# A gather's second half moved to another accumulator bank, and a branch hint for the tensor engine

## The chip, the cores and the metric

The kernel runs on one core of a Trainium2 chip. The metric is the device time of one execution in microseconds (us); a measurement is the median of several runs. One further execution is recorded by the hardware profiler, and every row shown here comes from such a record.

## What is computed

One layer of a decoder block for 512 tokens of width 1024, in float32:

```python
h = modulate(rms_norm(x, norm1_g), shift1, scale1)        # scales from the vector c
q, k, v, u, gates = split(h @ w_in)
x = x + gate1 * ((g_attn * (attention @ w_proj_attn) + g_ssm * (ssm @ w_proj_ssm)) @ w_out)
h = modulate(rms_norm(x, norm2_g), shift2, scale2)
# hierarchical mixture of experts: best of 4 groups, then best 2 of its 8 experts
hid = xb @ w_e_in[e]                # 32 experts, each 1024 x 1024
a, g = split(hid)
ys = (silu(a) * g) @ w_e_out[e]     # each 512 x 1024
x = x + gate2 * sum(weight * ys)
out = rms_norm(x, final_g)
```

The first two thirds of the text of the kernel compute the attention and state-space branches. The change is in the mixture of experts, the last 530 us of the execution.

## The kernel before

**Experts in pairs.** The 32 experts are worked through as 16 pairs, p = 0 to 15, with 64 places (CAP) for tokens in each expert. The weights of a pair come as 12 loads of 1 MiB (1,048,576 bytes): eight of `w_ein` (128 rows of both experts each) and four of `w_eout`. They go through a ring of 17 slots in the order in which they are used, so a load can be issued when the work that read the same slot 17 loads earlier has ended. `fetch` issues them on SyncE's queue.

**One pair on the tensor engine.** The order on TensorE and SyncE is the order of the program text (a manual schedule). VectorE and ScalarE are ordered by the framework's planner, until the last pair, from where they follow the text too. For each pair p TensorE does:

1. `hid_mm`, eight steps k: the pair's gathered tokens (`xT`) times `w_ein`, into `hid[0]` and `hid[1]`, which are PSUM banks 0 and 1.
2. `give(p - 1, ys[0], ...)`: four token blocks of the previous pair's first output half are put back to their tokens (8 matmuls, banks 4 to 7). VectorE adds them to x.
3. `gather`: the tokens of coming pairs are picked with a 0/1 matrix P (matmuls `xg`). One call of `gather` does one half of the width (four of the eight blocks of 128) for two pairs at once. Its output has two halves of 512 columns, and a half fills one bank: 16 matmuls, then a VectorE copy and a ScalarE copy into `xT`, one for each pair.
4. between the two halves, `act_turned`: four transposes of the activated `hid`, in bank 0, copied out by VectorE.
5. `places`: four small matmuls `ix` that find, for each place, its token and weight.
6. `give(p - 1, ys[1], ...)`, and then `yb_mm`: the second product, into `yb`, which is the tile `pair` on banks 2 and 3.

`gather` is called twice at p = 0 (both halves for pairs 1 and 2) and once at each of p = 1 to 12; at p = 13 it is called twice for the one pair that is left, where one bank holds the whole output (n = 1). In the kernel before, both halves of a call lie in one tile `both` on banks 2 and 3:

```python
both = pair((128, 2, per_bank, 128 * n) if n == 2 else (128, 2, 2, 128), name="xg")
for k0 in range(0, 4, per_bank):
    xg = both[:, k0 // per_bank] if n == 2 else both.rearrange("p a b c -> p (a b) c")
```

The framework places the waits between engines: an instruction that writes a PSUM tile waits for the ones that read what it overwrites, and two engines that read one tile are put one after the other. `places` has its output in bank 1.

**The end.** After pair 14 the last pair's `hid_mm` is interleaved with `give`, and its activation is transposed (L1540) and copied into `hT` by VectorE and ScalarE (L1541). Then every engine loads one number, the largest count of tokens of an expert (L1545), and branches on it (L1546): if a count is over 64, the body `overflow()` is run, a loop over all experts; here it is jumped over. The code behind the branch computes the last pair's output in five pieces (`piece`, matmuls `yq`, L1561), puts it back to the tokens, and normalizes and stores the result.

Of the kernel before, what the change touches and what calls it, by code (L numbers as in the profile page):

```python
# [20 lines left out]
KC = D // 128  # L21
NT = T // 128
NE = 32
CAP = 64
# [33 lines left out]
def hybrid_block(ctx: ExitStack, tc: tile.TileContext, x, cols, cst, ada_a, ada_b, b_rows, bc_rows, lamv, relb,  # L58
                 onehot, units, rw, rb, bpad, cpad, w_ein, w_eout, out):
    nc = tc.nc  # L60
    V, S, G, TE = nc.vector, nc.scalar, nc.gpsimd, nc.tensor
# [5 lines left out]
    def bank(i, shape=(128, 512), name=None):  # L67
        return psum.tile(list(shape), F32, tag=f"b{i}", name=name or f"bank{i}")
# [8 lines left out]
    def t1(tag, shape, dt=F32, name=None):  # L77
        pool = late if tag[:-1] == "tmp" else mid if tag[:-1] in ("BT", "CT", "sgA", "xs") else early
        return pool.tile(list(shape), dt, tag=tag, name=name or tag)
# [9 lines left out]
    def tt(o, a, b, op, eng=None):  # L89
        return emit(o, lambda: (eng or V).tensor_tensor(o, a, b, op=op))  # L90

    def ts(o, a, s1, op0, s2=None, op1=None, eng=None):
        return emit(o, lambda: (eng or V).tensor_scalar(o, a, s1, s2, op0=op0, **({"op1": op1} if op1 is not None else {})))  # L93
# [99 lines left out]
    def pair(shape=(128, 2, 512), name="pair"):  # L193
        return psum.tile(list(shape), F32, tag="b23", name=name)
# [324 lines left out]
    with tc.manual_schedule(engines={mybir.EngineType.PE, mybir.EngineType.DVE, mybir.EngineType.Activation}):  # L519
# [16 lines left out]
        for k in range(KC):  # L536
            first, second = unit_parts(UNITS[k]) if k in UNITS else (lambda: None, ) * 2
            for n in range(3 * 6):

                m, w = (n // 2, n % 2) if n < 12 else (n - 12, 2)  # L540
                b = 6 * k + m
# [431 lines left out]
    for i in range(4):  # L973
        m2s = []
        for m in (2 * i, 2 * i + 1):
# [5 lines left out]
            a = t1(f"u{m % 2}", [128, T], name="ma")  # L981
            b = t1(f"u{2 + m % 2}", [128, T], name="mb")
# [173 lines left out]
    def xg_mm(o, P, k, i, w, start):  # L1156

        TE.matmul(o, (h2h, h2l)[w][i][:, 128 * k:128 * k + 128], P[:, i].rearrange("p a b -> p (a b)"), start=start,  # L1158
                  stop=i == NT - 1 and w == 1, skip_group_check=True)
# [59 lines left out]
    with tc.manual_schedule(engines={mybir.EngineType.PE}):  # L1219
# [10 lines left out]
        for i in range(NT):  # L1230
            ps = bank((5, 0, 1, 0)[i], name="po2")
            n = T if i < 3 else 256
            for s_ in range(KC * T // n):
                k, c0 = s_ % KC, n * (s_ // KC)
# [14 lines left out]
    NP = NE // 2  # L1249
    ring = {}  # L1250
    nring = [-1]

    def slot(name, n=None, t=F32):
        if n is None:
            n = nring[0] = nring[0] + 1
        return p2r.tile([128, 2, D], t, tag=f"r{FREED[n % RING]}", name=name)
# [59 lines left out]
    xT, held, left = {}, {}, ["x0", "x1", "x2", "x3"]  # L1316

    def x_half(p, h):
        held[p, h] = left.pop(0)
        xT[p, h] = p2.tile([128, 4, 128], F32, tag=held[p, h], name="xT")  # L1320
        return xT[p, h]

    def gather(ps, P, h, between=None):

        n, per_bank = len(ps), 4 // len(ps)
        to = [x_half(p, h) for p in ps]
        both = pair((128, 2, per_bank, 128 * n) if n == 2 else (128, 2, 2, 128), name="xg")
        for k0 in range(0, 4, per_bank):
            xg = both[:, k0 // per_bank] if n == 2 else both.rearrange("p a b c -> p (a b) c")
            for kk in range(per_bank):  # L1330
                for i in range(NT):
                    for w in range(2):
                        xg_mm(xg[:, kk], P, 4 * h + k0 + kk, i, w, i == w == 0)
                if between and kk == 1 and k0 == 0:
                    between()
            for j in range(n):
                (V.tensor_copy, S.copy)[(j + k0 // per_bank) % 2](to[j][:, k0:k0 + per_bank], xg[:, :, 128 * j:128 * j + 128])  # L1337

    def places(p, P, j=0):

        ix = bank(1, (128, 6), "ix")
        for i in range(NT):
            TE.matmul(ix, P[:, i, 2 * j:2 * j + 2].rearrange("p a b -> p (a b)"), cwt[:, i, p], start=i == 0, stop=i == NT - 1)
        ws = p2.tile([128, 8], F32, tag="ws", bufs=4, name="ws")
        V.tensor_copy(ws[:, 0:6], ix)
        for e in range(2):
            r = slice(64 * e, 64 * e + 64)
            tt(ws[r, 6:7], ws[r, 2 * e:2 * e + 1], ws[r, 2 * e + 1:2 * e + 2], OP.add)
        ts(ws[:, 7:8], ws[:, 4:5], -1.0, OP.add)
        disp[p] = [ws]  # L1350
# [7 lines left out]
    def act(hid):  # L1358
        a = p2.tile([128, 512], F32, tag="hT", name="sa")
        S.activation(a, hid[0], AF.Silu)  # L1360
        tt(a, a, hid[1], OP.mult)
        return a
# [23 lines left out]
    def give(p, y, i, q, b):  # L1386

        ps = bank(b, name="cb")
        give_mm(p, y, i, ps)
        add(i, 512 * q, ps)  # L1390

    def hid_mm(p, hid, k):
        for q in range(2):
            for e in range(2):
                TE.matmul(hid[q][64 * e:64 * e + 64], xT[p, k // 4][:, k % 4, 64 * e:64 * e + 64], ring[p][k][:, e, 512 * q:512 * q + 512],  # L1395
                          start=k == 0, stop=k == KC - 1, skip_group_check=True)

    def yb_mm(p, yb, hT_, f):
        for q in range(2):
# [61 lines left out]
    for p in range(NP - 1):  # L1461
# [4 lines left out]
        hid = [bank(q, name="hid") for q in range(2)]  # L1466
        for k in range(KC):
            hid_mm(p, hid, k)
        a = act(hid)
# [4 lines left out]
        if p == 0:  # L1474
            with tc.issue_after(last[0].ins), tc.issue_after(last[1].ins):
                weights()
                P = chosen(1, 2)
            places(0, P0)
# [5 lines left out]
        if p == 0:  # L1484
            gather((1, 2), P, 0, act_turned)
            gather((1, 2), P, 1)
            places(1, P, 0)
            places(2, P, 1)
        elif p < NP - 3:
            if p % 2:  # L1490
                P = chosen(p + 2, 2)
                gather((p + 2, p + 3), P, 0, act_turned)
            else:
                gather((p + 1, p + 2), P, 1, act_turned)
            places(p + 2, P, 1 - p % 2)
        elif p == NP - 3:
            P = chosen(NP - 1, 1)
            gather((NP - 1, ), P, 0, act_turned)
            gather((NP - 1, ), P, 1)
            places(NP - 1, P)  # L1500
        else:
            act_turned()
# [11 lines left out]
    hid = [bank(q, name="hid") for q in range(2)]  # L1514
    for k in range(4):
        hid_mm(NP - 1, hid, k)
# [5 lines left out]
                                                  mybir.EngineType.Activation}))  # L1522

    for k in range(4, KC):
        hid_mm(NP - 1, hid, k)
        if k < KC - 1:
            for n in ((0, 1), (2, 3), (4, 5))[k - 4]:
                give(NP - 2, ys[n // 4], n % 4, n // 4, 4 + n % 2)
    a = slot("sa", free[0] + 3)[:, 0, :512]
# [13 lines left out]
        add(2 + j, 512, pl[j])  # L1543
    back(NP - 1, slot("PT", free[0] + 10, F32R)[:, 0, :512])
    ov = nc.values_load(ci[0:1, 0:1], min_val=0, max_val=2 * T)  # L1545
    with tc.If(ov > CAP):  # L1546
        overflow()

    PIECES = ((0, 256), (256, 256), (512, 256), (768, 128), (896, 128))
# [232 lines left out]
```

## Time and profile before

| | |
|---|---|
| median of 3 runs | 972.01 us (970.54 to 976.26) |
| the profiled execution's own time | 972.46 us |
| its span, first to last instruction | 970.3 us (2.16 us lie around it) |
| TensorE (PE) busy | 917.0 us, 95% |
| VectorE (DVE), ScalarE (ACT) busy | 501.4 us, 300.8 us |
| mean granted TensorE clock | 0.971 of full speed |
| moved by DMA | 267.66 MB |

In rows of the profile, PE stands for matmuls and PEld for TensorE's weight loads, PEq and PEldq for instructions of its sequencer. A row of a timeline has the start in us, the duration in us, the engine, the line, the operation with output and inputs, shapes and a count; what stands in brackets at its end is how long the engine had been idle before, and what ended that. Matmuls overlap: the next one starts before the one before has ended, so the distance of two starts is what one costs.

### The profile page before, as it was taken

What the parts mean: (1) busy time and instruction counts of PE and PEld (TensorE: products, weight loads), DVE (VectorE), ACT (ScalarE), POOL (GpSimd) and SP (SyncE); (2) the same over time, 40 slices, a digit from 0 to 9 for tenths busy, and PEclk for the clock granted to TensorE, in tenths of its full rate; (3) what the DMA queues carried; (4) which work ended last, traced back from release to release, by engine and by line L of the source; (5) the groups of instructions that cost most, each with busy time, mean ns of one, the idle gap of its engine ahead of it and who ended that gap; (6) DMA issues with size and microseconds to landing.
All of it is one profiled execution on the core that took longest, in us unless ns stands there. A gap on an engine that the chain in (4) does not pass through costs nothing. (4 is left out here: it accounts for less than half of the span.)

```text
span 970.3 us, 13070 instructions
## 1 busy us (share of the span) xinstructions
PE 917.0 (95%) x5060; PEld 571.3 (59%) x5060; DVE 501.4 (52%) x1249; ACT 300.8 (31%) x615; POOL 7.2 (1%) x12
## 2 busy tenths in 40 slices
PE   8997997989999999998899999999999999999985
PEld 5775764777877787786535553455544555446334
DVE  8886866756656565487204333343323444224236
ACT  4574588875545332243101010010100101000014
POOL 0000000000000000000000000000000000000002
PEclk9997998999999999997989999999999999999997
DMA  9925665421223433925878999999999999999902
GB/s 364 352 88 208 235 215 212 169 66 66 77 76 130 163 120 126 417 108 209 312 300 334 417 417 420 418 419 419 420 418 420 418 420 420 419 420 373 361 2 87
DMA packets 77189, 267.66 MB, mean 276 GB/s; under 512 B 5503, under 2 KB 11551, under 8 KB 77124
## 3 DMA queue, kind: packets, MB, share of 16 engines
q1 hardware_dynamic: 77124, 266.78, 70.4%
q8 instruction: 42, 0.69, 0.3%
q14 instruction: 23, 0.19, 0.1%
HBM read 264.64 MB, written 3.17 MB: 276 GB/s over the span
## 5 line engine op out<-in xcount | busy, mean ns | idle before, releaser
L1395 PE MATMUL hid<-w,xT 128*64 128x512 f32 x1024 | 225.2, 597 | 0.0
L1395 PEld LDWEIGHTS hid<-w,xT 128*64 128x64 f32 x1024 | 73.4, 138 | 146.5 <-issue 146.0
L1401 PE MATMUL yb<-w,sa 128*64 128x512 f32 x480 | 110.8, 616 | 0.0
L90 DVE TENSOR_TENSOR sa<-sa,hid 128x512 f32<-128x512 f32 (+1 forms) x17 | 11.1, 657 | 162.7 <-PE hid L1395 151.7
L90 DVE TENSOR_TENSOR wl<-ws,wh 128x1024 fp32r<-128x1024 f32 x52 | 63.5, 1222 | 55.0 <-ACT wh L153 44.3
L90 DVE TENSOR_TENSOR x<-x,cb 128x512 f32<-128x512 f32 (+1 forms) x132 | 79.9, 664 | 5.4 <-PE cb L1380 5.4
L180 PE MATMUL acc<-hh,wh 128*128 128x512 f32 x176 | 74.3, 422 | 4.4 <-ACT wh L153 4.4
L153 ACT ACTIVATE wh<-ws 128x1024 fp32r<-128x1024 f32 x51 | 53.7, 1057 | 78.1 <-PE acc L180 24.4
L1373 ACT CAST yh<-yf 128x512 fp32r<-128x512 f32 x29 | 18.0, 619 | 193.2 <-DVE yf L96 163.7
L1158 PE MATMUL xg<-P,mh 128*128 128x256 f32 (+1 forms) x288 | 67.7, 288 | 9.7 <-ACT xT L1337 7.3
L1401 PEld LDWEIGHTS yb<-w,sa 128*64 128x64 f32 x480 | 34.2, 141 | 68.7 <-issue 66.8
L180 PE MATMUL acc<-hl,wh 128*128 128x512 f32 x176 | 71.3, 405 | 0.0
L180 PE MATMUL acc<-hh,wl 128*128 128x512 f32 x176 | 71.1, 405 | 0.0
L96 DVE SCALAR_TENSOR_TENSOR yf<-yb,ws,gate 128x512 f32<-128x512 f32 x29 | 21.8, 751 | 90.8 <-PE yb L1401 90.3
L1158 PE MATMUL xg<-P,ml 128*128 128x256 f32 (+1 forms) x288 | 66.0, 282 | 0.0
L1360 ACT ACTIVATE sa<-hid 128x512 f32<-128x512 f32 x15 | 9.0, 597 | 169.5 <-PE hid L1395 169.5
L1158 PEld LDWEIGHTS xg<-P,mh 128*128 128x128 f32 x288 | 52.9, 192 | 13.9 <-ACT xT L1337 10.6
L1158 PEld LDWEIGHTS xg<-P,ml 128*128 128x128 f32 x288 | 53.0, 193 | 0.5
L1380 PE MATMUL cb<-yh,PT 128*128 128x512 f32 x116 | 48.4, 417 | 0.1
L1380 PE MATMUL cb<-yl,PT 128*128 128x512 f32 x116 | 45.8, 395 | 1.5 <-DVE yl L90 1.4
L180 PEld LDWEIGHTS acc<-hh,wh 128*128 128x128 f32 x176 | 34.0, 193 | 14.2 <-ACT wh L153 4.7
L180 PEld LDWEIGHTS acc<-hh,wl 128*128 128x128 f32 x176 | 33.9, 192 | 9.4 <-issue 1.6
(308 smaller groups left out, 1434.7 us busy)
## 6 DMA issues: line engine op xcount, KB each, us to landing
w<-w_ein SPq DMA_DIRECT2D x128, 1024.0 KB
w<-w_eout SPq DMA_DIRECT2D x63, 1024.0 KB
ws<-units SPq DMA_DIRECT2D x52, 512.0 KB
adaw<-ada_b SPq DMA_DIRECT2D x32, 512.0 KB
ada<-ada_a SPq DMA_DIRECT2D x8, 512.0 KB
ada<-ada_a SPq DMA_DIRECT2D x16, 256.0 KB
X<-x SPq DMA_DIRECT2D x4, 512.0 KB
x<-x SPq DMA_DIRECT2D x4, 512.0 KB
```

The source lines that it names most:

```text
L90: return emit(o, lambda: (eng or V).tensor_tensor(o, a, b, op=op))
L96: return emit(o, lambda: V.scalar_tensor_tensor(o, a, s, b, op0=op0, op1=op1, **k))
L153: return (lambda: S.activation(hi, st, AF.Copy) if u else V.tensor_copy(hi, st)), lambda: tt(lo, st, f32(hi), OP.subtract)
L180: TE.matmul(o, a, b, start=start and i == 0, stop=stop and i == 2)
L1158: TE.matmul(o, (h2h, h2l)[w][i][:, 128 * k:128 * k + 128], P[:, i].rearrange("p a b -> p (a b)"), start=start, stop=i == NT - 1 and w == 1 ...
L1360: S.activation(a, hid[0], AF.Silu)
L1373: S.copy(yh, yf)
L1380: TE.matmul(ps, PT if len(y) == 2 else f32(PT), a, start=w == 0, stop=w == len(y) - 1)
L1395: TE.matmul(hid[q][64 * e:64 * e + 64], xT[p, k // 4][:, k % 4, 64 * e:64 * e + 64], ring[p][k][:, e, 512 * q:512 * q + 512], start=k == 0 ...
L1401: TE.matmul(yb[q][64 * e:64 * e + 64], hT_[:, f, 64 * e:64 * e + 64], ring[p][8 + f][:, e, 512 * q:512 * q + 512], start=f == 0, stop=f == ...
```

## The change

- In `gather` the first half is written to a tile on banks 2 and 3 of which only the first bank is used, and the second half to a tile of its own in bank 1. With n = 1 nothing moves: the one output still lies in bank 2.
- In `places` the output `ix` moves from bank 1 to bank 0.
- After the matmuls of step k = 4 of the last pair's `hid_mm`, a hint is placed in TensorE's stream: the branch labelled "overflow" will likely be taken, that is, the body will be jumped over. Only TensorE gets it. `hid_mm` returns its last matmul so that the place can be named.

```diff
@@ gather
-        both = pair((128, 2, per_bank, 128 * n) if n == 2 else (128, 2, 2, 128), name="xg")
         for k0 in range(0, 4, per_bank):
-            xg = both[:, k0 // per_bank] if n == 2 else both.rearrange("p a b c -> p (a b) c")
+            xg = bank(1, (128, per_bank, 128 * n), name="xg") if k0 else pair((128, 8 // n, 128 * n), name="xg")
...
-                (V.tensor_copy, S.copy)[(j + k0 // per_bank) % 2](to[j][:, k0:k0 + per_bank], xg[:, :, 128 * j:128 * j + 128])
+                (V.tensor_copy, S.copy)[(j + k0 // per_bank) % 2](to[j][:, k0:k0 + per_bank], xg[:, :per_bank, 128 * j:128 * j + 128])
@@ places
-        ix = bank(1, (128, 6), "ix")
+        ix = bank(0, (128, 6), "ix")
@@ hid_mm
-                TE.matmul(hid[q][64 * e:64 * e + 64], ...)
+                m = TE.matmul(hid[q][64 * e:64 * e + 64], ...)
+        return m
@@ the last pair
-        hid_mm(NP - 1, hid, k)
+        mm = hid_mm(NP - 1, hid, k)
+        if k == 4:
+            with tc.issue_after(mm.ins):
+                tc.mark_branch_hint_location("overflow", "LikelyTaken", engines=[mybir.EngineType.PE])
...
-    with tc.If(ov > CAP):
+    with tc.If(ov > CAP, label="overflow"):
         overflow()
```

## Rows read from the trace of the kernel before

**Rows 1.** The page: TensorE's busy time and its share of the span.

```profile
PE 917.0 (95%) x5060; PEld 571.3 (59%) x5060; DVE 501.4 (52%) x1249; ACT 300.8 (31%) x615; POOL 7.2 (1%) x12
```

**Rows 2.** Windows: us, PE, PEld, DVE, ACT, POOL busy; granted clock; DMA share; GB/s.

```profile
529.80:859.90 330.10, 324.77 (x1674) 158.24 (x1672) 123.33 (x237) 28.40 (x55) 0.00 (x0) 1.00 1.02 418
...
859.90:920.00 60.10, 57.84 (x300) 27.82 (x298) 20.62 (x36) 3.67 (x6) 0.00 (x0) 1.00 1.00 389
920.00:944.40 24.40, 20.24 (x90) 7.56 (x86) 9.31 (x16) 3.69 (x6) 0.00 (x0) 1.00 0.01 3
```

**Rows 3.** Waits of TensorE: total us, times, longest us.

```profile
PE xg L1158 <- ACT xT L1337: 7.3, 14, 1.0
...
PE xg L1158 <- DVE xT L1337: 1.7, 2, 0.9
...
PE ix L1343 <- DVE sa L90: 0.7, 1, 0.7
```

**Rows 4.** Timeline of one gather's middle, all engines.

```profile
667.40 0.28 PE L1158 MATMUL xg<-P,ml 128*128 128x256 f32 x1
...
667.52 0.60 PE L1302 MATMUL xtp<-colt,sa 128*128 128x128 f32 x4
...
668.15 0.69 DVE L1306 COPY sa<-xtp 128x512 f32<-128x512 f32 x1
668.18 0.37 ACT L1337 COPY xT<-xg 128x256 f32<-128x256 f32 x1 [1.89 <-DVE xT L1337]
...
668.60 0.38 PE L1158 MATMUL xg<-P,mh 128*128 128x256 f32 x1 [0.49 <-ACT xT L1337]
668.83 0.28 PE L1158 MATMUL xg<-P,ml 128*128 128x256 f32 x1
...
672.32 0.42 DVE L1337 COPY xT<-xg 128x256 f32<-128x256 f32 x1
```

**Rows 5.** Timeline of TensorE in the two gathers at p = 0.

```profile
475.39 0.28 PE L1158 MATMUL xg<-P,ml 128*128 128x256 f32 x1
...
476.59 0.38 PE L1158 MATMUL xg<-P,mh 128*128 128x256 f32 x1 [0.92 <-DVE xT L1337]
...
478.46 0.28 PE L1158 MATMUL xg<-P,ml 128*128 128x256 f32 x1
...
479.72 0.38 PE L1158 MATMUL xg<-P,mh 128*128 128x256 f32 x1 [0.98 <-ACT xT L1337]
```

**Rows 6.** Timeline around the start of hid(13): TensorE, then VectorE.

```profile
859.95 13.90 PE L1395 MATMUL hid<-w,xT 128*64 128x512 f32 x64
```

```profile
861.65 0.69 DVE L90 TENSOR_TENSOR yl<-yf,yh 128x512 fp32r<-128x512 f32 x1 [0.74 <-ACT yh L1373]
```

**Rows 7.** Lines L1545 and L1546 on the sequencers: ns min/median/max, start us.

```profile
L1545 PEldq TENSOR_LOAD <-ci x1: 488/488/488, 939.7 to 939.7; - x1
```

```profile
L1546 PEldq COMPARE_BRANCH  x1: 3767/3767/3767, 940.3 to 940.3; - x1
...
L1546 ACTq COMPARE_BRANCH  x1: 50/50/50, 940.9 to 940.9; - x1
```

**Rows 8.** Timeline on both sides of the branch.

```profile
940.19 0.42 DVE L1541 COPY hT<-xtp 128x256 f32<-128x256 f32 x1 [0.52 <-PE xtp L1540]
...
944.39 5.36 PE L1561 MATMUL yq<-w,hT 128*64 128x256 f32 x32 [4.02 <-PEq L1546]
...
950.83 1.95 PE L1561 MATMUL yq<-w,hT 128*64 128x256 f32 x16
```

**Rows 9.** Windows of 2 us, columns as in rows 2.

```profile
488.00:490.00 2.00, 2.00 (x8) 0.71 (x6) 0.00 (x0) 0.00 (x0) 0.00 (x0) 0.50 0.00 0
...
946.00:948.00 2.00, 2.00 (x13) 1.36 (x11) 0.48 (x1) 0.14 (x1) 0.00 (x0) 0.50 0.00 0
...
950.00:952.00 2.00, 2.00 (x20) 1.51 (x20) 1.34 (x5) 0.96 (x4) 0.00 (x0) 1.00 0.00 0
```

**Rows 10.** DMA queues from 930 to 931 us: packets, MB, share of 16 engines.

```profile
q8 instruction: 1, 0.02, 8.4%
```

More of the change, by code (lines that the diff above doesn't have):

```diff
@@ L1394, in hid_mm @@
             for e in range(2):
-                TE.matmul(hid[q][64 * e:64 * e + 64], xT[p, k // 4][:, k % 4, 64 * e:64 * e + 64], ring[p][k][:, e, 512 * q:512 * q + 512],
-                          start=k == 0, stop=k == KC - 1, skip_group_check=True)
+                m = TE.matmul(hid[q][64 * e:64 * e + 64], xT[p, k // 4][:, k % 4, 64 * e:64 * e + 64], ring[p][k][:, e, 512 * q:512 * q + 512],
+                              start=k == 0, stop=k == KC - 1, skip_group_check=True)
+        return m
     def yb_mm(p, yb, hT_, f):
```

## The prediction

> **What bounds the kernel now.** I read the page first, then the windows of the mixture of experts, the waits of TensorE, the timeline of one gather, and last the rows around the branch. TensorE is busy for 95% of the span [rows 1]. From 529.80 to 859.90 us, which are eleven pairs of 30.0 us each, it is busy for 324.77 of 330.10 us at full clock, while the DMA engines are busy all the time too, at 418 GB/s [rows 2]. Two candidates, then, and the reader has to see which one sets the pace. A matmul that lacked its weights would show as TensorE waiting for a DMA; the list of waits has no such row for any expert weight, and its rows for these stages are those of [rows 3].
>
> How far ahead the loads are can be counted. All weights are 16 x 12 = 192 loads of 1.0486 MB, 201.3 MB. After 859.90 us there come 389 GB/s x 60.1 us = 23.4 MB, and then practically nothing [rows 2], so 177.9 MB or 169.7 loads had landed when hid(13) began at 859.95 [rows 6]. Thirteen pairs had used 156. So 13.7 of the ring's 17 slots held weights not yet used. The eleven pairs before took 132 loads, and 418 x 330.1 = 138.0 MB or 131.6 loads came in: the store was 14.1 at their start and hardly moves. The loads keep up, with about 34 us of them in hand (13.7 x 2.5 us). TensorE sets the pace, and time taken out of its stream comes off the end until that store is eaten.
>
> **The gather.** In the middle of a call TensorE stands still, although its next matmuls go to another bank than the one being copied. The last matmul of the first half starts at 667.40 and the four transposes at 667.52, so neighbours are about 0.12 us apart. The second half starts only at 668.60, 0.05 us after the ScalarE copy of the first half has ended (668.18 + 0.37), and that copy had itself waited for VectorE's [rows 4]. The one tile on two banks is what ties the second half to copies of the first. In the list this is the wait of xg for the ScalarE copy, 14 times and 7.3 us [rows 3]: 13 such places and one at p = 0 of another kind.
>
> The price of one place: the transposes start 0.11 apart ((0.60 - 0.27) / 3, the last one's length taken as 0.27), so the second half could start at 667.52 + 4 x 0.11 = 667.96 and starts 0.64 later. Its first matmul then takes 0.23 instead of 0.12, since its weights were not loaded ahead, which is another 0.11. Together 0.75 us; the bare idle time, 0.49, is the lower bound. With a bank of its own nothing holds the second half: bank 1 was `hid[1]`, read by VectorE before the gather began. 13 x 0.75 = 9.75 us (6.4 at the bound).
>
> At p = 0 the second call waits for the copies of the first call's second half, and its own second half for its first: 475.39 to 476.59 and 478.46 to 479.72 [rows 5]. Less the normal 0.12, and with the 0.11 for the first matmul, these are 1.19 and 1.25 us. With banks 2 and 1 in turn, each tile has a whole half (16 x 0.12 = 1.9 us) in which its two copies, 0.8 us together, are done. That is 2.4 us.
>
> **`places` in bank 0.** Its first call, at p = 0, waits 0.7 us for VectorE's read of `hid[1]` [rows 3]; bank 0 is read by ScalarE alone, earlier. I take 0.7 us, between nothing (if another input is as late) and that. Elsewhere bank 0 holds the transposes until VectorE has copied them, at 668.15 + 0.69 = 668.84 [rows 4]. `ix` follows the second half, from then on at about 667.96 + 1.9 = 669.85, so 1.0 us is left and the move is free; if VectorE were later than that, TensorE would wait for the difference. Sum for the first two edits: 9.75 + 2.4 + 0.7 = 12.9 us.
>
> Can it be kept? The store loses 12 x 0.75 = 9 us over the pairs 1 to 12, 3.6 loads at 2.5 us each; what is won at p = 0 moves the loads too, since slots come free earlier. A pair's low point is at the end of its `hid`, where 8 loads are used in 13.9 us and 5.5 come in. 13.7 - 3.6 - 2.5 = 7.6 loads remain. So it can.
>
> **The hint.** The same branch takes 50 ns on ScalarE and 3767 ns on TensorE [rows 7], whose body is the long one. Then `yq` starts, after 4.02 us of idle TensorE [rows 8], 0.3 us behind the end of the branch (940.3 + 3.77 = 944.07). With the code behind the branch at hand, the branch would cost the 0.05 us of the other engines. `yq` needs the first half of `hT`, which VectorE ends at 940.61 [rows 8], and would start at about 940.7: 3.6 us earlier. The trace has no row for a hint. It costs between nothing and, by the number that the same sequencer loads ahead of the branch, 0.49 us [rows 7]; it is executed while matmuls are queued, so I take 0.1. That is 3.5 us.
>
> What is late next? [...] 32 matmuls `yq` take 5.36 us behind the stall, 16 of the same shape 1.95 us at full clock [rows 8]. 5.36 - 3.90 = 1.4 us come back if the pause is only some tenths. Behind it TensorE's chain through the pieces stays the longest, and VectorE and ScalarE are idle up to it. 3.5 + 1.4 = 4.9 us.
>
> [...]
>
> **Sum.** 972.46 - 12.9 - 4.9 = 954.7 us, against the profiled execution's own time, which lies 0.45 us above the median of the runs.
>
> **Rivals.**
> - *The hint buys nothing.* The block fetched at 930 to 931 [rows 10] takes the place of the hinted one, and the branch costs 3.77 us again: 954.7 + 4.9 = 959.6 us. For it speaks that fetch; against it the ten microseconds between the hint and the branch, in which a block can come in.
> - *The loads take over.* The DMA share is 1.02 [rows 2]. If matmuls soon waited for weights, the pairs 1 to 12 would give back their 9 us: 963.7 us. Against it stands the store of 13.7 loads; it would need a store under 3.6 + 2.5 loads.
> - *The two halves stay tied*, by a wait that the list puts down to the wrong copy. Then only the end gains: 972.46 - 4.9 = 967.6 us. Against it: the second half starts 0.05 us behind a copy of the first, and the list puts all 14 waits down to that copy [rows 3].
> - *Slower: bank 1 now holds up `hid`.* The next pair's `hid[1]` must wait for the copies of the second half. VectorE makes its copy at 672.32 [rows 4], some 7 us before the next `hid`; its order is the planner's. If the copy were put behind `yl`, which starts at 861.65 for a `hid` that began at 859.95 [rows 6], `hid` would stall until 861.65 + 0.69 + 0.42 = 862.76. Its third matmul, the first in bank 1, is due at about 860.4, so that is 2.4 us, 14 times: 954.7 + 33.6 = 988 us. It turns the result from 17.8 / 14 = 1.3 us a gather on. Against it: the copy's inputs are ready long before, and nothing in front of it is late.
>
> **How the numbers follow.** The forecast as computed has 0.66, no gain from the hint 0.14, the loads 0.08, halves still tied 0.06, slower 0.03, and 0.03 is for mixtures between the second and the fourth. The forecast's own range is 951 to 958: up to 3.3 us more come off if the stretch around 488 us, at 0.50 clock [rows 9] behind the gathers of p = 0, becomes shorter (6.6 us at half clock lose 3.3); 3.4 us come back if one place is worth only 0.49. The range for the time goes from 950.5 to 964, and takes in the first two rivals. A measurement of this kernel can tell about 0.5%, 4.9 us, from no change; tied halves at 967.6 lie within that, the rest faster: 0.91, 0.06, 0.03.
>
> **What would show it.** Right: the wait of xg for the ScalarE copy is gone from the list but for the single-pair call at p = 13; a pair takes 29.25 us at a DMA share still near 1; the branch row of TensorE is near 0.05 us, `yq` starts some 0.4 us behind the transposes and no stretch behind it is at 0.50. Wrong: matmuls waiting for a DMA of w, `hid` or `ix` waiting for a VectorE copy, a branch of 3.7 us, or a fetch that stalls TensorE between hint and branch.

## The result, and the profile after

The changed kernel takes 959.9 us (median of 6, 957.84 to 960.65), the kernel before 973.6 us in the same series (median of 6). The ratio is 0.9854, with a 95% interval of 0.9829 to 0.9878: 1.2 to 1.7% faster. The time lies in the range of the prediction (950.5 to 964) and above the forecast's own range (951 to 958). The profiled execution took 959.85 us, with a span of 957.7 us.

The waits of TensorE, which answer to [rows 3], three rows from the list: total us, times, longest us.

```profile
...
PE row L1455 <- DVE x L90: 0.8, 1, 0.8
PE yq L1564 <- ACTq L1549: 0.8, 1, 0.8
PE xg L1158 <- DVE xT L1336: 0.8, 1, 0.8
```

The 14 waits for ScalarE's copy are gone, so are the wait of `ix` at p = 0 and one of the two for VectorE's copy. What is left of xg's wait for VectorE's copy is the call for a single pair at p = 13. No `hid` waits for a copy, and no matmul of the experts for a DMA.

The middle of a gather, timeline of all engines, which answers to [rows 4]:

```profile
660.14 0.28 PE L1158 MATMUL xg<-P,ml 128*128 128x256 f32 x1
660.26 0.60 PE L1302 MATMUL xtp<-colt,sa 128*128 128x128 f32 x4
660.46 0.42 DVE L1336 COPY xT<-xg 128x256 f32<-128x256 f32 x1
...
660.61 0.36 PE L1158 MATMUL xg<-P,mh 128*128 128x256 f32 x1
...
660.82 0.28 PE L1158 MATMUL xg<-P,ml 128*128 128x256 f32 x1
...
660.89 0.69 DVE L1306 COPY sa<-xtp 128x512 f32<-128x512 f32 x1
660.92 0.37 ACT L1336 COPY xT<-xg 128x256 f32<-128x256 f32 x1 [1.89 <-DVE xT L1336]
```

The second half starts 0.35 us behind the first transpose, while VectorE's copy of the first half still runs and ScalarE's has not begun; before it was 1.08 us (668.60 - 667.52 [rows 4]). That is 0.73 us a place. The first matmul still takes 0.21 us to the next start (its weight load starts 0.02 us ahead of it, those of the next ones 0.12 us ahead), so the 0.11 that the prediction added for it does not come back; but the second half starts 0.35 us behind the transposes where the prediction had 0.44, which makes up for nearly all of that.

The pairs, by the starts of their `hid` in TensorE's timeline, first of the changed kernel, then of the kernel before:

```profile
525.57 13.90 PE L1394 MATMUL hid<-w,xT 128*64 128x512 f32 x64
...
847.41 13.90 PE L1394 MATMUL hid<-w,xT 128*64 128x512 f32 x64
...
885.86 13.90 PE L1394 MATMUL hid<-w,xT 128*64 128x512 f32 x64
```

```profile
529.79 13.90 PE L1395 MATMUL hid<-w,xT 128*64 128x512 f32 x64
...
893.58 13.90 PE L1395 MATMUL hid<-w,xT 128*64 128x512 f32 x64
```

Eleven pairs, hid(2) to hid(13), take 847.41 - 525.57 = 321.84 us instead of 859.95 - 529.79 = 330.16: 8.32 us, or 0.76 a pair. The windows of that stretch and of the one where time was lost (us, PE, PEld, DVE, ACT, POOL busy; granted clock; DMA share; GB/s):

```profile
525.57:847.41 321.84, 321.84 (x1674) 157.96 (x1672) 123.32 (x237) 28.41 (x55) 0.00 (x0) 1.00 1.02 419
```

```profile
868.00:870.00 2.00, 1.93 (x15) 1.93 (x15) 0.02 (x1) 0.00 (x0) 0.00 (x0) 0.85 1.03 424
870.00:872.00 2.00, 2.00 (x11) 2.00 (x11) 0.00 (x0) 0.00 (x0) 0.00 (x0) 0.50 1.03 424
...
876.00:878.00 2.00, 2.00 (x6) 1.32 (x4) 1.67 (x3) 0.00 (x0) 0.00 (x0) 0.50 1.01 416
878.00:880.00 2.00, 2.00 (x7) 0.68 (x8) 1.31 (x3) 0.00 (x0) 0.00 (x0) 0.59 1.03 424
```

TensorE is busy for all of the 321.84 us, and the loads come in at the rate of before (419 GB/s, then 418). But hid(13) to hid(14) takes 885.86 - 847.41 = 38.45 us instead of 893.58 - 859.95 = 33.63. The work there is the same as before; the clock is not: from about 869.4 to 879.6 us it is granted at 0.50. That is 4.8 us lost, and no step of the prediction had it.

The branch and what follows, which answer to [rows 7, 8]: the line of the branch on TensorE's sequencer (ns), and the timeline.

```profile
L1549 PEldq COMPARE_BRANCH  x1: 412/412/412, 932.6 to 932.6; - x1
```

```profile
933.50 3.67 PE L1564 MATMUL yq<-w,hT 128*64 128x256 f32 x32 [0.82 <-ACTq L1549]
...
938.25 1.95 PE L1564 MATMUL yq<-w,hT 128*64 128x256 f32 x16
```

Where the 12.6 us between the two spans (970.3 and 957.7) are, from the starts of rows: up to hid(0) the changed kernel's execution is 1.9 us later (455.23 against 453.32), with the same order of work and clock falls in other places (170 to 180 us has a mean of 0.68, before 0.83); hid(0) to hid(1) gains 5.4 (36.50 against 41.90), hid(1) to hid(2) 0.7, hid(2) to hid(13) 8.3; hid(13) to hid(14) loses 4.8; the branch gains 3.2 (`yq` comes 13.67 us after the last pair's step k = 4 began, instead of 16.86); the matmuls behind it gain 1.7. -1.9 + 5.4 + 0.7 + 8.3 - 4.8 + 3.2 + 1.7 = 12.6.

### The profile page after: what moved, and what is told of

The parts are those of the page before. It is cut to its first block, busy times and chain, and to the rows that moved or that the text cites. A ratio compares the mean times of both kernels' runs of the same rounds, so it can differ in the third digit from the quotient of the medians.

```text
span 957.7 us, 13085 instructions
## 1 busy us (share of the span) xinstructions
PE 914.9 (96%) x5060; PEld 572.2 (60%) x5060; DVE 501.7 (52%) x1249; ACT 300.5 (31%) x615; POOL 7.2 (1%) x12
```

## The experiments

Kernels of one series ran on one chip beside the kernel before; ratios are to that, with 95% intervals. The theory: TensorE's stream sets the pace from the first pair to the end, each edit takes its own idle time out of it, and the loads have a store to lose.

### Each edit by itself

Gather and `places` without the hint:

```diff
-        if k == 4:
-            with tc.issue_after(mm.ins):
-                tc.mark_branch_hint_location("overflow", "LikelyTaken", engines=[mybir.EngineType.PE])
```

> The changed kernel without the hint: bank 1 for the gather's second half and bank 0 for ix stay. My theory (both edits pay, each in its own place, and they add): the branch takes about 3.77 us again and the matmuls yq behind it run partly at 0.50 clock, so the time is 4.9 us above the changed kernel: about 964.8 us, ratio to the kernel before 0.990; a pair still takes 29.26 us. Rival (the chain behind the branch has slack, so that the hint is worth less than its rows): within 1.5 us of the changed kernel, about 960 to 961 us.

Measured: 964.4 us, ratio 0.9906 (0.9886 to 0.9925). As expected: 4.5 us above the changed kernel.

The hint without the other edits (`both` and bank 1 for `ix` put back):

```diff
+        both = pair((128, 2, per_bank, 128 * n) if n == 2 else (128, 2, 2, 128), name="xg")
...
-        ix = bank(0, (128, 6), "ix")
+        ix = bank(1, (128, 6), "ix")
```

> The kernel before with the hint alone. My theory: the branch takes about 0.41 us, a pair still takes 30.0 us, and the time is 4.9 us below the kernel before: about 968.7 us, ratio 0.995. Rival (the hint only works because the gather edit moved the stream against the fetch blocks): the branch takes 3.7 us, ratio 1.000.

Measured: 970.22 us, ratio 0.9963 (0.9949 to 0.9977), which is 2.2 to 5.0 us, 3.3 by the medians. That is less than the 4.9 us expected, which lies at the edge of the interval; its runs go from 966.38 to 972.83 us. Its branch on TensorE's sequencer, and the one of the kernel without the hint:

```profile
L1550 PEldq COMPARE_BRANCH  x1: 407/407/407, 945.5 to 945.5; - x1
```

```profile
L1546 PEldq COMPARE_BRANCH  x1: 3712/3712/3712, 932.9 to 932.9; - x1
```

The hint works in either stream. In both, a pair takes what was expected of it: 29.26 us with the gather edit alone and 30.0 us with the hint alone. 9.1 us (973.48 - 964.4) and 3.3 us (973.48 - 970.22) add up to 12.4; both edits together gave 13.7 in their series, and 0.9906 x 0.9963 = 0.9869 lies within the interval of the changed kernel.

### The fall of the clock at p = 13

The changed kernel again, then a version in which the idle 0.78 us at p = 13 is taken away by giving the second single-pair call the other bank:

```diff
-            xg = bank(1, (128, per_bank, 128 * n), name="xg") if k0 else pair((128, 8 // n, 128 * n), name="xg")
+            xg = bank(1, (128, per_bank, 128 * n), name="xg") if k0 or (n == 1 and h) else pair((128, 8 // n, 128 * n), name="xg")
```

> The changed kernel once more, for a second trace. The question is the stretch at p = 13, which ran at 0.50 clock for 10 us in the first trace and cost 4.8 us. Theory A (the granted clock falls there in some executions and not in others, since nothing in the order of work differs from the kernel before): the fall may be missing here, or lie elsewhere, and hid(13) to hid(14) then takes 33.6 us as before; time 957 to 961 us. Theory B (the change itself brings it): hid(13) to hid(14) takes 38.4 us again.

> The changed kernel, and the second of the two single-pair calls at p = 13 also gets bank 1, so that its wait of 0.78 us for the copy of the first call goes. Theory A: 0.9 us less than the changed kernel, with or without a fall of the clock at p = 13: about 959.0 us. Theory C (the idle 0.78 us is what makes the clock fall at p = 13): no stretch at 0.50 there and 5.7 us less, about 954 to 955 us.

Measured: 959.9 us for the first (ratio 0.9867, 0.9845 to 0.9888), and its trace has the same fall. 954.22 us for the second, ratio 0.9806 (0.9785 to 0.9826), and the clock stays up. Windows of the second, the same stretch of time as above:

```profile
868.00:870.00 2.00, 2.00 (x20) 2.00 (x20) 0.00 (x0) 0.00 (x0) 0.00 (x0) 1.00 1.02 420
870.00:872.00 2.00, 2.00 (x12) 1.74 (x12) 1.82 (x7) 0.00 (x0) 0.00 (x0) 1.00 1.03 422
```

So taking away an idle time of 0.78 us, 0.9 us by the expectation, was worth 5.7 us. All three traces with the gather edit and the idle 0.78 us, the gather edit alone included, have the fall, and the two without the edit have not, although the same 0.78 us stands in them too. Either the edit's order of work brings the fall, or it depends on where in time the stretch lies. To tell these apart, I moved the stretch (the small `xg` matmuls at p = 13, called sparse in the expectations) with harmless work long before it: the transposes at p = 5 made four or seven times, 1.3 or 2.7 us (pair 5 takes 30.59 and 31.91 us with that, instead of 29.27).

```diff
-            for k in range(4):
+            for k in [*range(4)] * times:
                 TE.transpose(tp[:, k], src_[:, 128 * (q + k):128 * (q + k) + 128], ident)
...
-            turned_.append(act_turn(a, 0))
+            turned_.append(act_turn(a, 0, 4 if p == 5 else 1))
```

On the changed kernel:

> The changed kernel with the four transposes at p = 5 made four times instead of once: 12 x 0.11 = 1.3 us more of TensorE's time, nothing else changed, and everything behind it lies 1.3 us later. In three traces with the gather edit the clock fell to 0.50 at p = 13 (868 to 880 us), in two without it (the kernel before, and the hint alone) it did not, though the same 0.78 us of idle time stands there in all five. Theory A (whether it falls depends on where in time the sparse stretch at p = 13 lies): moved by 1.3 us it may stay at 1.00, and the time is 959.9 + 1.3 - 4.8 = 956.4 us. Theory B (the edit's own order of work brings the fall): it falls again, 961.2 us.

> The same with the transposes at p = 5 made seven times: 24 x 0.11 = 2.7 us later. Theory A: with one of the two shifts at least, no fall at p = 13; here then 959.9 + 2.7 - 4.8 = 957.8 us. Theory B: 962.6 us, and the fall is there.

Measured: with 1.3 us more work it takes 955.35 us, ratio 0.9826 (0.9790 to 0.9863); with 2.7 us more it takes 963.75 us, ratio 0.9901 (0.9868 to 0.9934). These two ran in one series and their runs do not overlap (954.96 to 956.91, 959.57 to 964.61). The changed kernel ran in another, on another chip: against the kernel before in each series, the smaller shift is 17.6 us faster and the changed kernel 13.6, so 1.3 us more work gains about 4.0 us, although the intervals of these two ratios overlap. Windows of the two shifts, first the smaller shift:

```profile
870.00:872.00 2.00, 2.00 (x21) 2.00 (x20) 0.00 (x0) 0.00 (x0) 0.00 (x0) 1.00 1.02 420
872.00:874.00 2.00, 2.00 (x12) 1.74 (x12) 1.82 (x7) 0.00 (x0) 0.00 (x0) 1.00 1.03 424
```

```profile
870.00:872.00 2.00, 1.71 (x15) 1.72 (x15) 0.23 (x1) 0.00 (x0) 0.00 (x0) 0.95 1.03 422
872.00:874.00 2.00, 2.00 (x11) 2.00 (x11) 0.00 (x0) 0.00 (x0) 0.00 (x0) 0.50 1.02 420
```

The granted clock is the number ahead of the DMA share: no fall with the smaller shift, the fall back with the larger one, as theory A has it. On the version without the idle time:

> The version whose second single-pair call has bank 1 (954.2 us, no fall at p = 13), with the transposes at p = 5 made four times. Theory C (that version is free of the fall since the idle 0.78 us is gone): no fall, 954.2 + 1.3 = 955.5 us. Theory A (it was free of it only by where the stretch lay): with this shift or the next the fall comes back, 955.5 + 4.8 = 960.3 us.

> The same with the transposes at p = 5 made seven times. Theory C: no fall at p = 13, 954.2 + 2.7 = 956.9 us. Theory A: the fall comes back here or with the smaller shift, 961.7 us.

Measured: 955.92 us (ratio 0.9824, 0.9788 to 0.9860) and 956.97 us (0.9841, 0.9806 to 0.9877), and neither trace has a fall at p = 13. So both theories hold in part.

The place can't be counted from the start of the execution, since the executions differ by some us ahead of hid(0): with the smaller shift hid(13) starts at 847.63 us, between the changed kernel (847.41) and the gather edit alone (847.69), and both of these fell. The idle 0.78 us is the same there. Windows and timeline, the changed kernel first, then the smaller shift:

```profile
517.90:521.20 3.30, 3.30 (x10) 0.97 (x8) 0.00 (x0) 0.00 (x0) 0.00 (x0) 0.50 0.58 230
```

```profile
868.07 0.33 PE L1158 MATMUL xg<-P,mh 128*128 128x128 f32 x1 [0.78 <-DVE xT L1336]
```

```profile
516.60:519.90 3.30, 3.30 (x10) 0.96 (x8) 0.00 (x0) 0.00 (x0) 0.00 (x0) 0.50 0.46 185
```

```profile
847.63 13.90 PE L1394 MATMUL hid<-w,xT 128*64 128x512 f32 x64
...
868.29 0.33 PE L1158 MATMUL xg<-P,mh 128*128 128x128 f32 x1 [0.78 <-DVE xT L1336]
```

Each of the two had its last fall ahead of hid(13) near the end of p = 1. Counted from where that fall starts, the stretch lies at a different place in the traces (us):

| version | last fall starts | hid(13) starts | from fall to hid(13) | idle 0.78 us at p = 13 | falls there |
|---|---|---|---|---|---|
| gather edit alone | 518.1 | 847.7 | 329.6 | yes | yes |
| changed kernel | 517.8 | 847.4 | 329.6 | yes | yes |
| changed kernel again | 517.2 | 847.4 | 330.2 | yes | yes |
| smaller shift | 516.5 | 847.6 | 331.1 | yes | no |
| larger shift | 516.8 | 849.6 | 332.8 | yes | yes |
| second call in bank 1 | 516.6 | 846.6 | 330.0 | no | no |
| kernel before | 522.0 | 860.0 | 338.0 | yes | no |

That the place decides is shown by the smaller shift, which keeps the edit, its order of work and the idle time. That the idle time decides too is shown by the second call in bank 1, which does not fall at a place between those where the changed kernel did (the late and the early hint below fell there too, at 330.2 and 330.1 us). Each of the two rests on one trace, with the times of the version's other runs agreeing. Of all nine traces with the edit and the idle 0.78 us (the four below included) eight have a fall there, and of the two without the edit none; but those two lie at other places (338.0 and 341.0 us), so whether the edit makes the fall likelier by more than the place is left open. Without the idle time the clock did not fall in three positions; three don't exclude that it does in a fourth.

### Why `ix` had to move

```diff
-        ix = bank(0, (128, 6), "ix")
+        ix = bank(1, (128, 6), "ix")
```

> The changed kernel with the output ix of places back in bank 1, where the gather's second half now lies too. My theory: ix must then wait until both copies of the second half are done, 0.37 us on ScalarE and 0.42 us on VectorE one after the other and about 0.2 us of hand-over, so TensorE idles about 1.0 us at each of 12 gathers and twice that order at p = 0: the edit's gain goes back, a pair takes 30.2 us, and the time is about 959.9 + 13 = 973 us (5 us less where the clock does not fall at p = 13). Rival (the move of ix is only tidying; something else, such as the four give matmuls behind it, covers the wait): no wait of ix in the list and 960 us.

Measured: 974.41 us, ratio 1.000 (0.9987 to 1.0013). Waits of TensorE:

```profile
PE ix L1342 <- DVE xT L1336: 12.0, 13, 0.9
...
PE ix L1342 <- DVE sa L90: 0.7, 1, 0.7
```

The wait for the copies is back, 12.0 us or 0.92 at each of 13 places: it is only handed from the second half to the next matmul that needs its bank. As expected in place. In size it is more: a pair takes 30.46 us (hid(2) to hid(13) 335.02), 1.20 more than in the changed kernel and 0.45 more than in the kernel before, where 30.2 was expected. That the time is no better than the kernel before, in spite of the hint, has two causes then: these eleven pairs take 4.9 us more than before, and hid(13) to hid(14) takes 36.85 us, 3.2 more than in [rows 6] and the row of hid(14) above, at a clock that falls there (0.50 from 888 to 894 us).

### Where the hint has to stand

Behind step k = 7 and behind step k = 0 of the last pair instead of k = 4:

```diff
-        if k == 4:
+        if k == KC - 1:
```

```diff
     for k in range(4):
-        hid_mm(NP - 1, hid, k)
+        mm = hid_mm(NP - 1, hid, k)
+        if k == 0:
+            with tc.issue_after(mm.ins):
+                tc.mark_branch_hint_location("overflow", "LikelyTaken", engines=[mybir.EngineType.PE])
```

> The changed kernel with the hint behind step k = 7 of the last hid instead of k = 4, about 1.5 us ahead of the branch instead of 11. My theory (the hint starts the fetch of the code behind the branch, and the branch waits for what is left of it): the branch takes 3.77 - 1.5 = 2.3 us, up to 0.4 if the sequencer comes to the hint while earlier matmuls are still queued; time 959.9 + 1.9 = 961.8 us. Rival (the hint only tells the branch which way to go, and the place does not matter): 0.41 us and 959.9 us.

> The changed kernel with the hint behind step k = 0 of the last pair's hid, some 25 us ahead of the branch and ahead of 96 more matmuls. My theory (the hinted block is kept until the branch): 0.41 us, 959.9 us. Rival, the one of the prediction (the blocks that the stream itself fetches in between take its place): the branch takes 3.7 us again, 964.8 us. In the trace of the kernel before one block came in at 930 to 931 us; at least one more block is passed in these 25 us.

Measured: late 964.38 us, ratio 0.9902 (0.9878 to 0.9927), early 959.16 us, ratio 0.9846 (0.9823 to 0.9870). The branch of each, late first:

```profile
L1549 PEldq COMPARE_BRANCH  x1: 3648/3648/3648, 932.2 to 932.2; - x1
```

```profile
L1549 PEldq COMPARE_BRANCH  x1: 407/407/407, 931.4 to 931.4; - x1
```

Early is as good as k = 4, as my theory had it. Late is worth nothing, where both theories expected a part or all of it. When TensorE's sequencer executes the hint stands in a row of its own; first the changed kernel, then late, then early:

```profile
L1781 PEldq BRANCH_PREFETCH_HINT  x1: 50/50/50, 917.3 to 917.3; - x1
```

```profile
L1781 PEldq BRANCH_PREFETCH_HINT  x1: 50/50/50, 926.8 to 926.8; - x1
```

```profile
L1781 PEldq BRANCH_PREFETCH_HINT  x1: 50/50/50, 903.1 to 903.1; - x1
```

The sequencer runs ahead of the matmuls: the hint is executed 15.3 us ahead of the branch in the changed kernel, 5.4 us in the late one and 28.3 us in the early one, not 11, 1.5 and 25 as the expectations counted. A fetch that starts at the late hint and takes as long as the branch without a hint, 3.7 us, would have been done by the branch; the branch takes 3648 ns all the same. So my theory of a fetch that starts at the hint does not hold there.

The windows of the instruction queue of [rows 10] show more. In the changed kernel a block comes in at 918.9 us, in the early one at 916.7, with the hint alone at 936.2, each between the hint and the branch. In the late one a block comes at 917.6, ahead of the hint, and then none until 933.2, when the branch already waits. It is so in all twelve traces with a hint: a block comes in between the hint and the branch in the eleven with a short branch (388 to 412 ns), and none in the one with a long branch. The queue in the changed kernel from 917.3 to 932.6 us, then all DMA in the late one from 926.8 to 932.2:

```profile
q8 instruction: 1, 0.02, 0.4%
```

```profile
DMA packets 0, 0.00 MB, mean 0 GB/s; under 512 B 0, under 2 KB 0, under 8 KB 0
```

One reading is that the hint decides what the next block is that the stream fetches anyway, and that the late hint came behind the last such fetch: the block came 13.6 us behind the early hint and 6.0 us behind the hint alone. The four versions with shifted work do not fit it as well: there a block came 0.4 to 4.4 us ahead of the hint and a further one 1.1 to 2.8 us behind it, as if the hint had started it. What is in a block can't be seen, so how the hint works is left open; what the traces show is that the branch was short wherever a block came in behind the hint.

### How far the loads' store goes

The second matmul of each `give`, the one with the low part `yl`, is left out for pairs 0 to 13 (so the experts' outputs are added back in the precision of their high part):

```diff
-        for w, a in enumerate(y):
+        used = y[:1] if p < NP - 2 else y
+        for w, a in enumerate(used):
...
-            TE.matmul(ps, PT if len(y) == 2 else f32(PT), a, start=w == 0, stop=w == len(y) - 1)
+            TE.matmul(ps, PT if len(y) == 2 else f32(PT), a, start=w == 0, stop=w == len(used) - 1)
```

> The changed kernel with the second matmul of each give, the one with the low part yl, left out for the pairs 0 to 13: 14 x 8 x 0.23 = 25.8 us less of TensorE's time, and nothing less to load. My theory (TensorE sets the pace and the loads have a store of some 14 slots to lose): a pair takes 29.26 - 1.84 = 27.4 us, the loads fall back 2.55 us a pair, 28 us over eleven pairs, which just empties the low point of the store, 11.5 slots or 29 us; so nearly all of it comes off, 934 to 940 us, with first waits for w near the end. Rival (the loads already set the pace at a DMA share of 1.02): a pair takes 30.0 us again or at least 29.3, and the time stays above 955 us.

Measured: 936.36 us, ratio 0.9618 (0.9588 to 0.9648). TensorE's timeline, starts of `hid`, and the first waits for weights:

```profile
577.27 13.90 PE L1395 MATMUL hid<-w,xT 128*64 128x512 f32 x64
...
604.68 13.90 PE L1395 MATMUL hid<-w,xT 128*64 128x512 f32 x64
...
809.33 1.94 PE L1395 MATMUL hid<-w,xT 128*64 128x512 f32 x8 [0.43 <-DMA w<-w_ein]
...
832.37 1.94 PE L1395 MATMUL hid<-w,xT 128*64 128x512 f32 x8 [0.52 <-DMA w<-w_ein]
```

A pair takes 27.41 us although its weights take 30 us to load, for ten pairs on end. The first wait comes in hid(12), at 809 us, at the end of a `hid`, the low point that was counted; in hid(13) each step from the fifth on waits half a microsecond, which is the pace of the loads (2.5 us against 1.94). So the store was there, about as large as counted, and by hid(13) it is used up: more time taken from TensorE in these pairs should only lengthen the waits for weights, which no run here shows.

## Why the prediction was right

**The bound** was right, and shown by the last experiment: TensorE sets the pace beside loads that run at a share of 1.02. With it the rival in which the loads take over fell. The one in which bank 1 holds up `hid` fell by the list of waits, and the one in which the halves stay tied by the second half's start.

**The gather** was right: 0.76 us a pair, against 0.75. That the size is so close is in part luck, since the 0.11 us for the first matmul did not come and the second half started 0.09 us earlier than the prediction had it. At p = 0 the three waits and that of `ix` went as forecast; hid(0) to hid(1) gained 5.4 us, 1.5 more than the 0.75 + 2.4 + 0.7 of the waits there. By the durations of their stretches, 1.25 of that is clock: `yb` gave 1.2 (8.78 against 9.96 us), the `row` matmuls 0.45 (2.05 against 2.50), and `hid` took 0.4 back (16.20 against 15.82). The granted clock is 0.50 from 484 to 487 us, before it was from 485 to 491. The prediction had the shorter stretch at 0.50 only as the lower end of its range.

**`places`** was right that the move costs nothing, and did not say what the move is for: without it there is no gain at all (ratio 1.000), as the run with bank 1 shows.

**The hint** was right in kind. The branch takes 0.41 us, not 0.05, and the stall gave 3.2 us, not 3.5 (3.6 by the prediction's own numbers, since 944.39 - 940.7 is 3.7). The clock behind the branch came back as forecast: 32 matmuls `yq` take 3.67 us instead of 5.36, 1.7 us against 1.4, and all windows from 932 to 946 us are granted at 1.00 (before, 944 to 946 us had 0.81 and 948 to 950 us 0.84, on both sides of the 0.50 in [rows 9]); only the last 6 us of the execution are at 0.50, as the last 8 were before, with no matmul in them. The rival, a hint that loses its block to the next fetch of the stream, fell: a block does come in between the hint and the branch in every hinted version with a short branch. With a hint and such a block the branch takes 388 to 412 ns; in the gather edit alone, without a hint, it takes 3712 ns, and a block comes in while it lasts (at 933.9, the branch having begun at 932.9). That the branch waits for this block is my reading; no row shows what is in it.

**What was off** is a missing term in the sum: the clock of the stretch at p = 13, which the prediction put at nothing. It took for granted that the clock stays up wherever it was up before, and counted the clock only where a stall was removed. The stretch of small matmuls at p = 13, moved earlier, fell to 0.50 for ten microseconds and cost 4.8 us: 954.7 + 4.8 = 959.5, beside 959.85 of the profiled execution. So the time lies 1.9 us above the forecast's own range and inside the wider one, which had been widened for two rivals that did not come about. That the other small misses cancel is chance: 1.9 us lost ahead of hid(0), 1.5 more gained at p = 0 than forecast. The versions in which the stretch did not fall took 954.2 us (without the idle time) and 955.35 us (moved by 1.3 us). That the work behind p = 0 moves against the clock's falls could have been seen beforehand; whether a fall would come or go could not have been worked out from one trace.

The best version found is the changed kernel with the other bank for the second single-pair call: 954.22 us, 2.0% below the kernel before.

## What to carry to other kernels

The tile on two accumulator banks tied the write of one bank to the readers of the other here (14 waits, 7.3 us [rows 3]), and a bank of its own untied them (none of the 14 is left); but look at who is the next to use that bank, for the wait can go there (12.0 us of `ix` in the run with bank 1). Before believing that DMA engines at a share of 1.02 set the pace, count the loads that have landed and are not yet used: a store of 14 slots let TensorE gain 28 us from hid(2) to hid(13) (302.3 us in the last experiment, 330.2 before) with the first waits for weights only at the end. And where a kernel has a stretch of small matmuls with idle time in it, a saving elsewhere can be eaten by a fall of the clock there, as 4.8 us were here, and a small saving in the stretch itself can be worth several times its size, as 0.78 us of idle time were worth 5.7 here; a shift by harmless work tells such a loss from a real one.

## What was not expected of the hardware

- Adding 1.3 us of work made the kernel about 4 us faster (955.35 us, 17.6 below the kernel before, against 959.9, 13.6 below), since the stretch at p = 13 then kept its clock (1.00, where the changed kernel had 0.50). With 1.3 us more still, the fall was back (963.75 us). The stretch has the same work and the same idle time in all three.
- A hint that TensorE's sequencer executes 5.4 us ahead of the branch is worth nothing (3648 ns), and one 28.3 us ahead all (407 ns): what the short branches have in common is a block of instructions that came in between.
